# Sum of ReLU over rows: the first chunk in four loads of every fourth partition, and two row blocks instead of three

## The chip, the core and the metric

The kernel runs on one core of one Trainium2 chip. It uses ScalarE (ACT), VectorE (DVE) and SyncE (SP), which issues all transfers; TensorE has no part in it. The metric is the device time of one execution in microseconds, the median of several. The profile is one execution, taken by the hardware profiler; its times count from the start of its first instruction.

## The reference

```python
batch, seq, dim = 32, 512, 1024
x = np.random.randn(batch, seq, dim).astype(np.float32)

def reference(x):
    relu_x = np.maximum(x, 0)
    return np.sum(relu_x, axis=-1).astype(np.float32)
```

The input is 16384 rows of 1024 float32 numbers, 64 MB; the output is one number per row, 64 KB. Every number is read once.

## The kernel before

The rows are dealt to the 128 partitions of the on-chip buffer, 128 rows to each. `REGIONS = [1, 111, 16]` cuts the input into three row blocks. In a block of n, partition p holds the n consecutive rows from p*n on: in the first block one row (the first 128 rows of the input are contiguous over the partitions), in the second 111 rows (so that partition starts lie 444 KB apart), in the third 16 rows (64 KB apart).

Seven chunks of 16 rows per partition (64 KB per partition, 8 MB in all) go through three buffers of `buf`. Chunk 0 comes by two loads at L91, one of the first block's row (4 KB of each partition, 512 KB in all) and one of 15 rows of the second block (60 KB of each partition, 7680 KB in all). Chunks 1 to 6 are one load of 64 KB per partition each. All loads of a chunk count up the same semaphore, `s_in[c]`, by 16 each. The two loads of chunk 0 are moved in the instruction list ahead of SP's part in the start barrier, so they are issued first of all; chunks 1 and 2 follow behind the barrier, chunks 3 to 6 and the tail each wait until the DVE has finished with the buffer that they need (`s_dve`). The third block is the tail: loads of 8, 4 and 2 rows (L101), and two last rows in four pieces (three at L112, one at L115), one of which goes into a small buffer, `seam`.

On chunks 0 to 5, ACT applies ReLU in place to several rows at a time (L145) and the DVE sums them row by row into `res` (L160); in chunk 5 four rows are done outright by one engine each. From chunk 6 on, ACT (L127) and DVE (L130) take rows in turn, each with ReLU and sum in one operation. `res` has one column for each of the 128 rows of a partition.

The result goes out by three stores. Column 0 belongs to the first block, whose 128 results are contiguous in the output: after chunk 1 the DVE transposes the first 32 columns of `res` into `turned` (L169), and SP stores four rows of 32 numbers from there (L117). SP reaches this store behind all loads. The second block's 111 columns are stored at L123, once the last load of L112 has landed and chunk 6 is done, the third block's 16 columns at L207, once the last two sums are there. The program ends when all stores have landed.

Of the kernel before, what the change touches and what calls it, by code (L numbers as in the profile page):

```python
# [3 lines left out]
P = 128  # L4
D = 1024
BIG = 16
NB = 3
REGIONS = [1, 111, 16]
CHUNKS = [[(0, 0, 1), (1, 0, 15)]] + [[(1, 16 * c + 15, 16)] for c in range(6)]
ACT_STEPS = [[16], [7, 9], [7, 9], [7, 9], [4, 5, 7], [3, 4, 5]]  # L10
DVE_STEPS = [[4, 5, 7], [7, 4, 5], [7, 4, 5], [7, 4, 5], [4, 5, 7], [3, 4, 5]]
TAIL = [8, 4, 2]
# [4 lines left out]
def bass_relu_sum_kernel(  # L17
# [14 lines left out]
    fp32 = mybir.dt.float32  # L32
# [5 lines left out]
    J = B * S // P  # L38
    NBIG = len(CHUNKS)
    assert BIG * NBIG + sum(TAIL) + 2 == J == sum(REGIONS)  # L40

    xr = x.rearrange("b s d -> (b s) d")
    of = out.rearrange("b s -> (b s)")
    start = [sum(REGIONS[:i]) for i in range(len(REGIONS))]
    xv = [
        xr[P * s : P * (s + n), :].rearrange("(p j) d -> p j d", p=P)
        for s, n in zip(start, REGIONS)
    ]
    ov = [of[P * s : P * (s + n)].rearrange("(p j) -> p j", p=P) for s, n in zip(start, REGIONS)]

    buf = nc.alloc_sbuf_tensor("buf", [P, NB, BIG, D], fp32)
    w = D - CUT
    seam = nc.alloc_sbuf_tensor("seam", [P, 2 + w + HEAD + 2], fp32)
    res = nc.alloc_sbuf_tensor("res", [P, J], fp32)
    turned = nc.alloc_sbuf_tensor("turned", [P, 32], fp32)

    n_in = NBIG + len(TAIL) + 3
    s_in = [nc.alloc_semaphore(f"s_in{i}") for i in range(n_in)]
    s_act = nc.alloc_semaphore("s_act")
    s_dve = nc.alloc_semaphore("s_dve")  # L60
# [2 lines left out]
    s_half = nc.alloc_semaphore("s_half")  # L63
    s_seam = nc.alloc_semaphore("s_seam")
    s_last = nc.alloc_semaphore("s_last")
    s_turn = nc.alloc_semaphore("s_turn")
    s_store = nc.alloc_semaphore("s_store")
    s_out = nc.alloc_semaphore("s_out")

    sp, act, dve = nc.sync, nc.scalar, nc.vector  # L70

    NTWO = len(ACT_STEPS)
    done = [sum(map(len, DVE_STEPS[: c + 1])) for c in range(NTWO)]
# [5 lines left out]
    code = nc.main_func.blocks[0].instructions  # L79
    arrival = next(  # L80
        i
        for i, ins in enumerate(code)
        if ins.engine == mybir.EngineType.SP and type(ins).__name__ == "InstDrain"
    )
    for c in range(NBIG + 1):
        if c >= NB:
            sp.wait_ge(s_dve, done[c - NB])
        if c < NBIG:
            i = 0
            for g, j, n in CHUNKS[c]:  # L90
                sp.dma_start(  # L91
                    out=buf[:, c % NB, i : i + n, :], in_=xv[g][:, j : j + n, :]
                ).then_inc(s_in[c], 16)
                i += n
                if c == 0:
                    code.insert(arrival, code.pop())
                    arrival += 1
    r = 0
    tail = []
    for i, n in enumerate(TAIL):  # L100
# [10 lines left out]
    for k, (lo, hi) in enumerate((first, second, third)):  # L111
# [1 line left out]
            s_in[NBIG + len(TAIL) + k], 16  # L113
        )
    sp.dma_start(out=seam[:, 2 : 2 + w + HEAD], in_=rows[:, CUT : D + HEAD]).then_inc(s_seam, 16)  # L115
    sp.wait_ge(s_turn, 1)
    sp.dma_start(  # L117
        out=of[0:P].rearrange("(k q) -> k q", q=32), in_=turned[0:P:32, 0:32]
    ).then_inc(s_store, 16)
    sp.wait_ge(s_fact, 1)  # L120
    sp.wait_ge(s_fdve, 1)
    sp.wait_ge(s_in[-1], 16)
    sp.dma_start(out=ov[1][:, :], in_=res[:, start[1] : start[2]]).then_inc(s_store, 16)  # L123


    def on_act(t, acc):
        return act.activation(t, t, AF.Relu, accum_out=acc)  # L127

    def on_dve(t, acc):
        return dve.tensor_scalar(  # L130
            out=t, in0=t, scalar1=0.0, scalar2=None, op0=ALU.max, op1=ALU.add, accum_out=acc
        )

    def row(c, i):
        return buf[:, c % NB, i, :], res[:, c * BIG + i : c * BIG + i + 1]

    k = 0
    for c in range(NTWO):
        alone = BIG - sum(ACT_STEPS[c])
        act.wait_ge(s_in[c], 16 * len(CHUNKS[c]))  # L140
        r = 0
        ready = []
        for n in ACT_STEPS[c]:
            t = buf[:, c % NB, r : r + n, :]
            act.activation(t, t, AF.Relu).then_inc(s_act, 1)  # L145
            k += 1
            ready += [k] * n
            r += n
        for i in range(BIG - alone // 2, BIG):
            on_act(*row(c, i))  # L150
        if alone:
            dve.wait_ge(s_in[c], 16 * len(CHUNKS[c]))
            for i in range(BIG - alone, BIG - alone // 2):
                on_dve(*row(c, i))
        r = seen = 0
        for n in DVE_STEPS[c]:
            if ready[r + n - 1] > seen:
                seen = ready[r + n - 1]
                dve.wait_ge(s_act, seen)
            dve.tensor_reduce(  # L160
                out=res[:, c * BIG + r : c * BIG + r + n],
                in_=buf[:, c % NB, r : r + n, :],
                axis=X,
                op=ALU.add,
            ).then_inc(s_dve, 1)
            r += n
        if c == 1:
            dve.wait_ge(s_dve, done[c])
            dve.transpose(out=turned[:, :], in_=res[:, 0:32]).then_inc(s_turn, 1)  # L169


    j0 = NBIG * BIG
    for c in range(NTWO, NBIG):
        act.wait_ge(s_in[c], 16 * len(CHUNKS[c]))
        dve.wait_ge(s_in[c], 16 * len(CHUNKS[c]))
        for i in range(BIG):
# [15 lines left out]
    k = 2 + w  # L192
# [14 lines left out]
    sp.dma_start(out=ov[-1][:, :], in_=res[:, start[-1] : J]).then_inc(s_out, 16)  # L207
    sp.wait_ge(s_store, 16 * (len(REGIONS) - 1))
    sp.wait_ge(s_out, 16)
# [28 lines left out]
```

## Time and profile before

| | us |
|---|---|
| median of 3 runs | 160.88 (160.72 to 160.93) |
| span of the profiled execution, first to last instruction | 159.4 |
| DVE busy | 120.6 (76%) |
| ACT busy | 101.5 (64%) |
| input read, 67.11 MB, over the span | 421 GB/s |
| idle time of ACT until loads landed, L145 | 46.1 in 6 waits, 19.1 the longest |

The profiled execution's own time is its span; what a timed run has around it is the difference, 1.5 us. Instructions are named by engine, line, operation and tiles. "SPq" is SP's issuing of transfers; a load's "us to landing" counts from the start of its issue to its completion, including the time that it stands in the queues behind others.

### The profile page before, as it was taken

Reading aid. Unit: us, or ns where it says so; the run is one execution under the profiler, and the core shown is the slowest. Engines: PE = TensorE matmul, PEld = TensorE weight load, DVE = VectorE, ACT = ScalarE, POOL = GpSimd, SP = SyncE. Lnnn points to the kernel's source line nnn. Section 1 sums busy time; section 2 is a strip of 40 time slices with the busy share of each in tenths; the row PEclk is TensorE's granted clock in tenths of the full one; section 3 lists DMA queues with packets and bytes.
Section 4 is the critical chain, followed back from the end, with each engine's and each line's share of the span. In section 5 each row is a group of like instructions: output and inputs, shape, how many; then the busy total and the mean of one; then the engine's idle time right before and its main releaser. Section 6 shows DMA issues by size and latency. Waiting matters only on the chain.

```text
span 159.4 us, 150 instructions
## 1 busy us (share of the span) xinstructions
DVE 120.6 (76%) x59; ACT 101.5 (64%) x54; POOL 0.2 (0%) x4
## 2 busy tenths in 40 slices
DVE  0000000009999999999999999999999999898995
ACT  3000059980799708996099941999329980496975
POOL 0000000000000000000000000000000000000000
DMA  9997996996996997989979969969969979798994
GB/s 378 493 401 339 493 526 263 526 526 263 526 493 296 526 444 345 526 378 411 526 312 477 526 263 526 526 263 526 526 263 526 444 345 526 321 469 374 417 400 142
DMA packets 2457, 67.18 MB, mean 421 GB/s; under 512 B 536, under 2 KB 792, under 8 KB 1176
## 3 DMA queue, kind: packets, MB, share of 16 engines
q1 hardware_dynamic: 2456, 67.18, 98.1%
q14 instruction: 1, 0.01, 0.0%
HBM read 67.11 MB, written 0.07 MB: 421 GB/s over the span
## 4 chain that ended last, share of the span: by engine, by line
DVE 55%; DMA 34%; ACT 9%; SPq 2%; issue 0%
DVE res L160 54%; DMA buf<-in_x_dram 34%; ACT buf L145 9%; SPq L101 1%; SPq L112 1%; DVE buf L130 0%; DVE seam L130 0%; SPq L91 0%; DVE turned L169 0%
## 5 line engine op out<-in xcount | busy, mean ns | idle before, releaser
L160 DVE TENSOR_REDUCE res<-buf 128x4 f32<-128x4096 f32 (+3 forms) x18 | 99.4, 5596 | 35.5 <-ACT buf L145 35.5
L145 ACT ACTIVATE buf<-buf 128x7168 f32<-128x7168 f32 (+5 forms) x13 | 80.4, 6233 | 46.1 <-DMA buf<-in_x_dram 46.1
L127 ACT ACTIVATE buf<-buf 128x1024 f32<-128x1024 f32 (+2 forms) x19 | 19.0, 999 | 8.9 <-DMA buf<-in_x_dram 8.9
L130 DVE TENSOR_SCALAR_CACHE_REDUCE buf<-buf 128x1024 f32<-128x1024 f32 (+2 forms) x19 | 20.7, 1143 | 1.7 <-DMA buf<-in_x_dram 1.6
L127 ACT ACTIVATION_READ_ACCUMULATOR buf<-buf 128x1 f32 x19 | 3.6, 188 | 0.0
L145 ACT ACT_TABLE_LOAD x1 | 1.3, 1283 | 1.3 <-PEq L223 1.3
L130 DVE DVE_READ_ACCUMULATOR buf<-buf 128x1 f32 x19 | 1.6, 84 | 0.0
L130 DVE TENSOR_SCALAR_CACHE_REDUCE seam<-seam 128x258 f32<-128x258 f32 x1 | 0.4, 421 | 0.0
L127 ACT ACTIVATE seam<-seam 128x114 f32<-128x114 f32 x1 | 0.3, 300 | 0.1
L169 DVE STREAM_TRANSPOSE turned<-res 128x32 f32<-128x32 f32 x1 | 0.2, 211 | 0.0
L127 ACT ACTIVATION_READ_ACCUMULATOR seam<-seam 128x1 f32 x1 | 0.2, 186 | 0.0
L223 POOL MEMSET const-bfloat16-1.0<- 128x1 bf16 x1 | 0.1, 101 | 0.0
L223 POOL MEMSET const-uint8-127<- 128x1 uint8 x1 | 0.1, 101 | 0.0
L223 POOL MEMSET const-float32-0.0<- 128x1 f32 x1 | 0.1, 98 | 0.2 <-issue 0.2
L223 POOL MEMSET const-float32-1.0<- 128x1 f32 x1 | 0.1, 98 | 0.0
L130 DVE DVE_READ_ACCUMULATOR seam<-seam 128x1 f32 x1 | 0.1, 82 | 0.0
## 6 DMA issues: line engine op xcount, KB each, us to landing
buf<-in_x_dram SPq DMA_DIRECT2D x1, 7680.0 KB, 21.1
buf<-in_x_dram SPq DMA_DIRECT2D x1, 4096.0 KB, 25.3
buf<-in_x_dram SPq DMA_DIRECT2D x1, 2048.0 KB, 29.9
buf<-in_x_dram SPq DMA_DIRECT2D x1, 1024.0 KB, 31.9
buf<-in_x_dram SPq DMA_DIRECT2D x1, 512.0 KB, 3.3
buf<-in_x_dram SPq DMA_DIRECT2D x1, 456.0 KB, 32.5
buf<-in_x_dram SPq DMA_DIRECT2D x1, 256.0 KB, 32.7
seam<-in_x_dram SPq DMA_DIRECT2D x1, 184.0 KB, 32.6
```

What stands on the lines that cost most here:

```text
L101: sp.dma_start(out=buf[:, tb, r : r + n, :], in_=xv[-1][:, r : r + n, :]).then_inc(s_in[NBIG + i], 16)
L112: sp.dma_start(out=flat[:, lo:hi], in_=rows[:, lo:hi]).then_inc(s_in[NBIG + len(TAIL) + k], 16)
L127: return act.activation(t, t, AF.Relu, accum_out=acc)
L130: return dve.tensor_scalar(out=t, in0=t, scalar1=0.0, scalar2=None, op0=ALU.max, op1=ALU.add, accum_out=acc)
L145: act.activation(t, t, AF.Relu).then_inc(s_act, 1)
L160: dve.tensor_reduce(out=res[:, c * BIG + r : c * BIG + r + n], in_=buf[:, c % NB, r : r + n, :], axis=X, op=ALU.add,).then_inc(s_dve, 1)
L169: dve.transpose(out=turned[:, :], in_=res[:, 0:32]).then_inc(s_turn, 1)
L223: nc = _bacc.Bacc("TRN2", target_bir_lowering=False, num_devices=1)
```

## The change

There are two row blocks, `REGIONS = [112, 16]`: partition starts of the first lie 448 KB apart. All seven chunks are 16 rows of the first block. Chunk 0 comes by four loads; load q brings 64 KB to each of the partitions q, q+4, q+8, ..., 32 partitions each. All four are placed ahead of SP's part in the start barrier, and ACT waits for all four (64 counts). The transpose, its buffer, its semaphore and its store are gone; the store at the end takes 112 columns.

```diff
-REGIONS = [1, 111, 16]
-CHUNKS = [[(0, 0, 1), (1, 0, 15)]] + [[(1, 16 * c + 15, 16)] for c in range(6)]
+REGIONS = [112, 16]
+CHUNKS = [[(0, 16 * c, 16)] for c in range(7)]
+STEPS = [[4]] + [[1]] * 6
...
-            for g, j, n in CHUNKS[c]:
-                sp.dma_start(
-                    out=buf[:, c % NB, i : i + n, :], in_=xv[g][:, j : j + n, :]
-                ).then_inc(s_in[c], 16)
+            for (g, j, n), step in zip(CHUNKS[c], STEPS[c]):
+                for q in range(step):
+                    sp.dma_start(
+                        out=buf[q::step, c % NB, i : i + n, :], in_=xv[g][q::step, j : j + n, :]
+                    ).then_inc(s_in[c], 16)
+                    if c == 0:
+                        code.insert(arrival, code.pop())
+                        arrival += 1
                 i += n
-                if c == 0:
-                    code.insert(arrival, code.pop())
-                    arrival += 1
...
-    sp.wait_ge(s_turn, 1)
-    sp.dma_start(
-        out=of[0:P].rearrange("(k q) -> k q", q=32), in_=turned[0:P:32, 0:32]
-    ).then_inc(s_store, 16)
     sp.wait_ge(s_fact, 1)
     sp.wait_ge(s_fdve, 1)
     sp.wait_ge(s_in[-1], 16)
-    sp.dma_start(out=ov[1][:, :], in_=res[:, start[1] : start[2]]).then_inc(s_store, 16)
+    sp.dma_start(out=ov[0][:, :], in_=res[:, 0 : start[1]]).then_inc(s_store, 16)
...
-        act.wait_ge(s_in[c], 16 * len(CHUNKS[c]))
+        act.wait_ge(s_in[c], 16 * sum(STEPS[c]))
...
-        if c == 1:
-            dve.wait_ge(s_dve, done[c])
-            dve.transpose(out=turned[:, :], in_=res[:, 0:32]).then_inc(s_turn, 1)
```

More of the change, by code (lines that the diff above doesn't have):

```diff
@@ L54, in bass_relu_sum_kernel @@
     res = nc.alloc_sbuf_tensor("res", [P, J], fp32)
-    turned = nc.alloc_sbuf_tensor("turned", [P, 32], fp32)
     n_in = NBIG + len(TAIL) + 3
@@ L65, in bass_relu_sum_kernel @@
     s_last = nc.alloc_semaphore("s_last")
-    s_turn = nc.alloc_semaphore("s_turn")
     s_store = nc.alloc_semaphore("s_store")
@@ L151, in bass_relu_sum_kernel @@
         if alone:
-            dve.wait_ge(s_in[c], 16 * len(CHUNKS[c]))
+            dve.wait_ge(s_in[c], 16 * sum(STEPS[c]))
             for i in range(BIG - alone, BIG - alone // 2):
```

## The prediction

> **What bounds the kernel now.** I read the page first, then its part on DMA issues, the timeline, the table of stretches and the chain, and at the end the trace's record of single DMA packets for the first microseconds.
>
> The DMA row of the slices and the timeline (start us, us, engine, line, operation, tile, idle before it) settle the bound:
>
> ```profile
> span 159.4 us, 150 instructions
> DMA  9997996996996997989979969969969979798994
> ...
> 21.61 13.86 ACT L145 ACTIVATE buf<-buf 128x16384 f32<-128x16384 f32 x1 [19.06 <-DMA buf<-in_x_dram]
> 40.97 13.95 ACT L145 ACTIVATE buf<-buf 128x7168 f32<-128x7168 f32 x2 [5.50 <-DMA buf<-in_x_dram]
> 60.31 13.95 ACT L145 ACTIVATE buf<-buf 128x7168 f32<-128x7168 f32 x2 [5.39 <-DMA buf<-in_x_dram]
> 70.11 0.21 DVE L169 STREAM_TRANSPOSE turned<-res 128x32 f32<-128x32 f32 x1
> 137.72 1.22 DVE L130 TENSOR_SCALAR_CACHE_REDUCE buf<-buf 128x1024 f32<-128x1024 f32 x1 [0.42 <-DMA buf<-in_x_dram]
> 157.01 0.42 DVE L130 TENSOR_SCALAR_CACHE_REDUCE buf<-buf 128x256 f32<-128x256 f32 x1 [0.40 <-DMA buf<-in_x_dram]
> ```
>
> Every chunk of 8 MB is awaited by ACT, and chunks land 19.36, 19.34, ... us apart. The stretches (from:to, length, busy time of each engine, clock, DMA share, GB/s) say that nothing else limits that pitch:
>
> ```profile
> 21.60:40.97 19.37, 5.47 (x2) 13.86 (x2) 0.00 (x0) 1.00 1.00 433
> 40.97:60.31 19.34, 19.34 (x4) 13.95 (x3) 0.00 (x0) 1.00 1.00 434
> 60.31:79.67 19.36, 19.32 (x6) 13.96 (x3) 0.00 (x0) 1.00 1.00 433
> ```
>
> The queues are full (share 1.00) at 433.5 GB/s, 19.35 us a chunk. The DVE is as full, but as a follower: it starts when ACT has done chunk 0 and has 0.42 us to spare when chunk 6 lands at 137.72. The page's chain walks through the DVE and says otherwise:
>
> ```profile
> DVE 55%; DMA 34%; ACT 9%; SPq 2%; issue 0%
> ```
>
> It goes from the last data back to their issue at L101 (122.07), which waited for a DVE reduction. That is a wait of the issuing queue, not of the data: chunk 6 was still arriving until 137.72, so the tail's loads stood in the queue for some 15 us. The real chain is: start of the first load, 64 MB at a constant rate, 2.4 us of closing work. So the time moves one for one with the moment from which **all** DMA engines stream, and the change works there.
>
> The beginning, from the page's DMA issues (KB, us to landing):
>
> ```profile
> buf<-in_x_dram SPq DMA_DIRECT2D x1, 7680.0 KB, 21.1
> buf<-in_x_dram SPq DMA_DIRECT2D x1, 512.0 KB, 3.3
> ```
>
> Chunk 0 is complete at 21.59; a chunk takes 19.35 in the stream, so 2.24 us are start-up. The 512 KB load (4 KB of each partition) would take 1.21 us at the stream's rate and landed after 3.3: 2.1 us are issue, first access and landing. 7680 KB are 18.14 us, 3.3 + 18.14 = 21.44: another 0.15 was lost behind it.
>
> The packet record opens the 2.24 up. A packet is one partition's contiguous run, eight per DMA engine and load. The sixteen engines start their first 4 KB packet between 1.01 and 1.34 us. Those first packets last 362 ns on average, the others 175, the shortest 159; 4 KB at 27.1 GB/s (64 KB in 2418 ns) would be 151. The engines begin their 60 KB packets between 2.50 and 2.94 us, and this stagger of about 0.5 us stays to the end: the completion marks of chunk 0 arrive from 21.07 to 21.59, those of chunk 5 from 117.84 to 118.34. The slowest engine decides. The 60 KB packets last 2267 ns at best, the eight of one engine together lose 0.18 us to this.
>
> **The change, part by part** (gain positive, in us, for the slowest engine).
>
> 1. *No 4 KB packets.* Each engine now gets two 64 KB packets from each of four loads, 8 x 64 KB as before. Eight times the 8 ns of a small packet go: +0.06. The small packets' mutual delay, 7 x (175 - 159) ns, goes: +0.11. Bounds 0 and 0.31 (all that the 4 KB packets lost against 159 ns). The wait of each engine's first packet, 362 - 159 = 0.20, stays: 0.
> 2. *First load of 32 rows instead of 128.* The stagger of 0.33 between the engines' first packets may come from handing out eight rows to each engine in turn. With two rows it lies between 0.33 (no gain) and a quarter, 0.08 (gain 0.25). The stores at the end, eight rows per engine on a running queue, end within 0.14 to 0.15 us over all engines; so rows are part of it, not all. I take half: +0.13.
> 3. *Issue on SP.* Loads at L91 take 0.33 to 0.50 us; the one transfer whose partitions are stepped, the turned store at L117, took 0.63. If the step is what costs, each first packet comes 0.24 later than with the 0.39 of today's first issue. The four loads at 0.33 to 0.50 resemble the load rows more than a four-row store: 0, the loss end is -0.24. The second load is needed only when the first's two packets are through (4.8 us after its start), the others later; at 0.45 us apart they are queued by about 1.8 us.
> 4. *Two issues more ahead of SP's part in the start barrier*: the barrier ends some 0.9 us later. Behind it wait the table load of ACT (at 1.27, with 19.06 us of idle time after it) and the issue of chunk 1 (now at 1.28, needed at 20.7). Cost 0; without that cover 0.9.
> 5. *Two more completion marks per engine*, 9 ns each, with at most 0.03 for a change of load (19.35 less eight packet pitches of 2.4145): -0.02, end -0.06.
> 6. *Rows start 448 KB apart instead of 444.* The nearest row is the tail, 64 KB apart: all 128 of its 32 KB packets took exactly 1213 ns. The 64 KB packets of today's chunks take 2421 on average against 2418 at best, 0.03 per chunk. So 0 taken, gain end 0.16, loss end -0.18 (the excess of the cold first rows once more). That excess of 0.18 itself stays, since the first rows touched are again far apart.
> 7. *The transpose goes* (0.21 us at 70.11 and its wait on the DVE's own results). The DVE's slack at 137.72 grows from 0.42 to about 0.6; ACT and SP don't wait on it. 0. If the chunks came 0.4 faster with the DVE unmoved, the DVE would be late next; but it moves with chunk 0.
> 8. *The turned store goes from SP's queue* (0.63 at 125.35). Behind it SP only waits for the end's data, 31.0 us long. Its four 128 B packets lay behind all loads. 0. The 111 columns become 112: that store is issued at 157.08 and complete by 159.05, the last one, issued at 157.93, lands at 159.35 and sets the end. 0.
>
> Sum: 0.06 + 0.11 + 0.13 - 0.02 = 0.28. The span of 159.4 becomes 159.1. The timed median, 160.88 (160.72 to 160.93), has 1.5 us around the span that I leave alone: **160.6**. A change below 0.2%, 0.32 us, can't be told from none here.
>
> No row shows how 32 stepped partitions are dealt to the engines; the table of stretches has only full loads, at 433.5 GB/s. [...]
>
> **The rivals.**
>
> *A (slower): two engines share a way into the buffer during the first chunk.* In today's full loads each engine runs at 27.1 GB/s with no neighbour in its way. If the dealing of 32 rows sends two engines to partitions with one common path, both get half. Price: four loads at half rate are 38.7 instead of 19.35, 180 us in all; one load in four shared would be +4.8. It decides as soon as more than 0.6 us is lost (0.28 + 0.32): a quarter of one 64 KB packet of 2.42 us is then enough sharing. For it: nothing in the trace shows this shape. Against: the four loads together give every partition once, and the step of four spreads each of them over the whole buffer.
>
> *B (no gain): the start is latency.* First access (0.20), stagger (0.33) and issue remain, and the stepped issue costs 0.1 to 0.24: gain 0.17 less that, about 160.8.
>
> *C (more gain): the first packet comes sooner*, because fewer rows have to be prepared. The last 8 KB store lands 1.4 us after issue, so of 2.24 at most 0.84 can go: 160.0. With the full quarter stagger and the 0.16 of point 6: 160.3.
>
> **How the numbers follow.** Forecast case (sum between 0.15 and 0.45): 0.47, nearly split by the bound of 0.2%. C: 0.18. B, with small losses: 0.25. A: 0.10. Faster by over 0.2%: 0.18 + 0.22 = 0.40. Within: 0.25 of the forecast case + 0.17 of B = 0.42. Slower: 0.08 + 0.10 = 0.18. The range takes in B with its issue and row ends (160.88 + 0.24 + 0.06, about 161.2) and C to 160.1; it leaves out A and the edges, under 0.2.
>
> **What would show it.** Right: no 4 KB packets, the engines' first marks of the fourth load between 20.8 and 21.3, ACT's first operation at about 21.3 instead of 21.61, later pitches 19.35, everything behind moved by the same amount. Step 2 is wrong if the first packets still start over 0.33 us; step 3 if the first L91 issue takes over 0.5; step 6 if pitches leave 19.35. A would show as a first operation of ACT near 41, with DMA GB/s near 217 in the first slices. If ACT's first operation moves and the end doesn't, the DVE or the tail is the bound, and this reading is wrong.

## The result and the profile after

The changed kernel takes 161.82 us (five runs, 161.54 to 162.10) against 160.88 (160.72 to 160.93): slower, ratio 1.0062, 95% interval 1.0050 to 1.0073. That is 0.94 us more where 0.28 less was forecast, and beyond the upper end of the range. Ratios here and below hold fast runs against fast runs; only two runs of one variant, the 60 KB load stepped, are left out as slow.

The profiled execution has a span of 160.0 instead of 159.4, so 0.6 us of the loss lie inside it. The rest lies outside. The prediction took 1.5 us around the span from a median and the span of one execution; run by run, time less span is 1.36 us on average before (1.3 to 1.4 in fifteen runs) and 1.79 after (1.64 to 1.86 in five). So there are two losses to find: 0.56 us at the first chunk, 0.43 us around the span.

The page of the changed kernel (span, and the DMA row of the slices in tenths), answering to the lines shown of before:

```profile
span 160.0 us, 150 instructions
...
DMA  7997997999979969969969969969969979798994
```

It is as full as it was, but for the first slice (7 instead of 9). The timeline (start us, us, engine, line, operation, tile, idle before it):

```profile
22.17 13.86 ACT L141 ACTIVATE buf<-buf 128x16384 f32<-128x16384 f32 x1 [17.78 <-DMA buf<-in_x_dram]
41.49 6.18 ACT L141 ACTIVATE buf<-buf 128x7168 f32<-128x7168 f32 x1 [5.47 <-DMA buf<-in_x_dram]
...
138.25 1.22 DVE L126 TENSOR_SCALAR_CACHE_REDUCE buf<-buf 128x1024 f32<-128x1024 f32 x1 [0.61 <-DMA buf<-in_x_dram]
...
157.55 0.42 DVE L126 TENSOR_SCALAR_CACHE_REDUCE buf<-buf 128x256 f32<-128x256 f32 x1 [0.42 <-DMA buf<-in_x_dram]
```

ACT's first operation comes at 22.17 instead of 21.61, 0.56 later. From there nothing is won or lost: 41.49 is 0.52 later, 138.25 is 0.53, the last sums at 157.55 are 0.54. The stretches between chunks are as full as before:

```profile
22.16:41.49 19.33, 5.43 (x2) 13.86 (x2) 0.00 (x0) 1.00 1.00 434
41.49:60.85 19.36, 19.36 (x4) 13.95 (x3) 0.00 (x0) 1.00 1.00 433
```

The chain in order of time (start us, length, what) shows where the start went:

```profile
0.00 0.55 SPq L91
0.55 0.06 issue
0.60 0.58 SPq L91
1.18 0.04 issue
1.22 0.59 SPq L91
1.81 0.04 issue
1.86 20.29 DMA buf<-in_x_dram
```

Each stepped load takes 0.55 to 0.59 us to issue. The record of single packets adds that the sixteen DMA engines begin their first packet between 1.32 and 1.82 us (before: 1.01 to 1.34), and that these first 64 KB packets last 3.12 us on average where 2.418 is the best and the usual one: 0.70 lost by each engine on average. Before, a first 4 KB packet lost 0.20.

The second loss has its sign in the page's queue lines. Before:

```profile
q1 hardware_dynamic: 2456, 67.18, 98.1%
q14 instruction: 1, 0.01, 0.0%
```

After:

```profile
q1 hardware_dynamic: 2352, 67.18, 97.9%
```

Before, one packet of 8 KB of instructions was fetched within the span (at 159.21, the span ends at 159.39). After, no such packet is in it; the record has two, at 161.31 and 161.59, after the last profiled instruction at 159.96.

### The profile page after: what moved, and what is told of

It reads as the page before. It is cut to its first block, busy times and chain, and to the rows that moved or that the text cites. A ratio compares the mean times of both kernels' runs of the same rounds, so it can differ in the third digit from the quotient of the medians.

```text
span 160.0 us, 150 instructions
## 1 busy us (share of the span) xinstructions
DVE 120.4 (75%) x58; ACT 101.5 (63%) x54; POOL 0.2 (0%) x4
## 4 chain that ended last, share of the span: by engine, by line
DVE 55%; DMA 33%; ACT 9%; SPq 2%; issue 0%
DVE res L156 54%; DMA buf<-in_x_dram 33%; ACT buf L141 9%; SPq L91 1%; SPq L101 1%; SPq L112 1%; DVE buf L126 0%; DVE seam L126 0%
```

## The experiments

The table gives the runs. Medians are to be held against 160.81 to 160.88 of the kernel before, measured along with them. "Beyond" is time less span, the mean over the runs; "first packet" the start of the earliest one; "lost" what the engines' first packets lost on average against the best packet of the same size. All but the median and "beyond" come from one profiled execution each. Two pairs begin with the same loads, so they show how far single profiles scatter: ACT starts at 21.81 and 21.95 with one load, at 21.73 and 22.23 with 4 KB first, 448 KB apart.

| kernel | median | beyond | first issue at SP | first packet | lost | ACT starts |
|---|---|---|---|---|---|---|
| before | 160.86 | 1.36 | 0.39 | 1.01 | 0.20 | 21.61 |
| after | 161.82 | 1.79 | 0.55 | 1.32 | 0.70 | 22.17 |
| one load instead of four | 161.42 | 1.80 | 0.37 | 1.01 | 0.68 | 21.81 |
| two loads, every second partition | 161.76 | 1.73 | 0.55 | 1.34 | 0.61 | 22.05 |
| four loads of 32 neighbours | 183.24 | 1.90 | 0.39 | 1.02 | 2.54 | 43.27 |
| 4 KB first, 448 KB apart | 161.46 | 1.79 | 0.38 | 1.01 | 0.31 | 21.73 |
| before, 60 KB load stepped behind the 4 KB | 162.09 | 1.37 | 0.40 | 1.03 | 0.2 | 23.38 |
| before, 60 KB load first | 161.44 | 1.35 | 0.39 | 1.02 | 0.73 | 22.34 |
| before, a touch of the rows | 161.05 | 1.46 | 0.39 | 1.02 | 0.2 | 21.85 |
| after, two waits more on the DVE | 161.46 | 1.38 | 0.54 | 1.33 | 0.70 | 22.15 |
| 4 KB first, 448 KB apart, two waits more on the DVE | 161.08 | 1.38 | 0.38 | 1.01 | 0.45 | 22.23 |
| after, two waits more on ACT | 161.88 | 1.87 | 0.55 | 1.34 | 0.64 | 22.22 |
| one load, two waits more on the DVE | 161.05 | 1.37 | 0.37 | 1.00 | 0.71 | 21.95 |
| before, two DVE instructions less | 161.05 | 1.59 | 0.39 | 1.02 | 0.17 | 21.62 |

### One load instead of four

```diff
-STEPS = [[4]] + [[1]] * 6
+STEPS = [[1]] * 7
```

> The changed kernel with chunk 0 as one load of all 128 partitions, 64 KB each; blocks of 112 and 16 rows, no turned store. Three theories of the 0.56 us that ACT's first operation moved back (21.61 to 22.17). Issue: the stepped loads are slow to issue (0.55 us against 0.39), so the first packet comes at 1.32 instead of 1.01; here the issue is 0.33 to 0.42 and the first packet starts at 1.01. Cold: sixteen engines that begin with 64 KB packets in rows far apart lose 0.7 us each in the first packet (2418 ns at best); here the first packets still last 3.0 us or more, and ACT starts at 21.6 to 21.8. Crowding: the first packets are slowed by three more loads being prepared while they run; here they last under 2.6 us and ACT starts at about 21.2.

161.42 us, ratio to before 1.0041 (1.0029 to 1.0053). The issue is back at 0.37 and the first packet at 1.01; the first packets still last 3.09 us. ACT:

```profile
21.81 13.86 ACT L141 ACTIVATE buf<-buf 128x16384 f32<-128x16384 f32 x1 [19.76 <-DMA buf<-in_x_dram]
```

So stepping costs 0.36 at ACT (22.17 less 21.81) and 0.40 in the median. The long first packets are there with a single load, so crowding by the three others falls. What remains of ACT's delay against before is 0.20, with a first packet of 64 KB in place of the small contiguous load.

### Two loads of every second partition

```diff
-STEPS = [[4]] + [[1]] * 6
+STEPS = [[2]] + [[1]] * 6
```

> The changed kernel with two loads of every second partition instead of four of every fourth. Issue theory: the issue is slow because partitions are stepped, 0.55 us again, first packet at 1.3. If the issue's cost came from having fewer rows than 128, it would lie between 0.39 and 0.55. Cold theory: first packets last 3.0 us or more, ACT at 22.0 to 22.2. Crowding theory: one more load instead of three, ACT at about 21.8. The start barrier ends about 1.2 us earlier than with four loads; if the time beyond the span hangs on it, it lies between 1.5 and 1.8.

161.76 us (1.0053; 1.0041 to 1.0065). The issues take 0.55 and 0.57 with 64 rows as with 32. The chain in order of time begins so:

```profile
0.00 0.55 SPq L91
0.55 0.06 issue
0.61 21.42 DMA buf<-in_x_dram
```

The earlier barrier changes nothing beyond the span (1.73).

### Four loads of 32 neighbouring partitions

```diff
-                        out=buf[q::step, c % NB, i : i + n, :], in_=xv[g][q::step, j : j + n, :]
+                        out=buf[P // step * q : P // step * (q + 1), c % NB, i : i + n, :],
+                        in_=xv[g][P // step * q : P // step * (q + 1), j : j + n, :],
```

> The changed kernel with four loads of 32 neighbouring partitions instead of every fourth. Issue: if 0.55 us come from stepping the partitions, these issues take 0.33 to 0.42; if they come from 32 rows, 0.55 again. Sharing (rival A of the prediction, at its proper place): if engines share ways by neighbouring partitions, the packets last 4.8 us instead of 2.42, ACT starts near 41 and the span is 179; if not, ACT starts at 21.8 to 22.2.

183.24 us in two runs. Two things come apart here. The issues take 0.39 to 0.42 although they have only 32 rows each, one of them 0.52 when issued as the fourth. The chain begins so:

```profile
0.00 0.39 SPq L91
0.39 0.06 issue
0.44 0.42 SPq L91
0.86 0.04 issue
0.90 0.42 SPq L91
```

So the slow issue goes with the step (0.55 to 0.59 with 32 rows, 0.55 and 0.57 with 64), not with the number of rows. And here is the half rate of rival A of the prediction: the packets of the first chunk last 4.91 to 5.12 us on average instead of 2.42, and the slices show it (GB/s in 40 slices):

```profile
GB/s 231 231 231 231 231 217 202 58 217 419 289 448 462 462 462 462 462 419 303 433 462 462 462 462 462 419 303 433 462 462 462 462 462 419 303 433 462 394 391 155
```

In its timeline ACT starts at 43.27:

```profile
43.27 13.86 ACT L142 ACTIVATE buf<-buf 128x16384 f32<-128x16384 f32 x1 [39.70 <-DMA buf<-in_x_dram]
```

The first chunk runs at about half rate (231 GB/s against 433.5), later ones, over all partitions, at the full one (433 on average from the tenth to the 33rd slice). What the engines share in it, if anything, no run shows. The change's step of four has no such loss: from their third packet on, its engines lose nothing (2418 to 2422 ns).

### 4 KB first, in rows that lie apart

```diff
-CHUNKS = [[(0, 16 * c, 16)] for c in range(7)]
-STEPS = [[4]] + [[1]] * 6
+CHUNKS = [[(0, 0, 1), (0, 1, 15)]] + [[(0, 16 * c, 16)] for c in range(1, 7)]
+STEPS = [[1, 1]] + [[1]] * 6
```

> The changed kernel's blocks of 112 and 16 rows and no turned store, but chunk 0 by two loads over all partitions as before the change, 4 KB and then 60 KB of each partition; the first 4 KB now lie 448 KB apart instead of one behind the other. Cold theory: the 4 KB packets meet the far-apart rows first and last 0.5 us or more longer in all; the first load lands at 3.8 or later instead of 3.3 and ACT starts at 21.9 to 22.2. Issue and crowding theories: as before the change, landing at 3.3, ACT at 21.6, time within 0.2% of 160.88.

161.46 us (1.0036; 1.0024 to 1.0048). The first load lands at 3.63, 0.3 later than the contiguous one and less late than the cold theory said; then the 60 KB packets lose nothing at all (2267 to 2272 ns, against 0.18 us per engine before). Sum of both: ACT at 21.73, between the 21.61 of before and the 21.81 of one large load. Single profiles are too coarse to rank these starts, so the mean spans over all runs decide. They are 159.6 for this kernel and 159.7 for the one with one large load, and 159.7 for both when the DVE has two waits more, against 159.5 before. So small or large, a first load in rows that lie apart costs these kernels the same, 0.2 against before. Most of this kernel's loss of 0.6 us is again beyond the span.

### The 60 KB load stepped behind the contiguous one

```diff
+STEPS = [[1, 4]] + [[1]] * 6
...
-            for g, j, n in CHUNKS[c]:
...
+            for (g, j, n), step in zip(CHUNKS[c], STEPS[c]):
+                for q in range(step):
...
```

> The kernel before (blocks of 1, 111 and 16 rows, turned store), whose 60 KB load alone is replaced by four loads of every fourth partition; the contiguous 512 KB load stays first. Issue theory: the slow issues are hidden behind the first load's packets, ACT starts at 21.6 to 21.7. Crowding theory: the 60 KB packets start while loads are still being issued and lose 0.5 us or more, ACT starts at 22.1. Cold theory: as the issue theory. If the 0.3 us by which the changed kernel's timed runs grew beyond its span come from the later start barrier, the median grows by 0.3 here too although the span stays.

None of the three theories' numbers came. The ten runs scatter from 160.97 to 163.75, with a median of 162.09 and spans of 159.6 to 162.4; without the two longest the ratio is 1.0059 (1.0035 to 1.0084). In the profiled one (162.40) ACT starts at 23.38. Its fourth stepped issue took 1.27 us, and three engines began their 60 KB packets between 3.89 and 4.57 us, when the other thirteen had begun by 3.14; they stayed late to the end. What held them was not found. The expectation's last sentence is answered: the barrier ended 3.0 us later than before (ACT's table load at 4.24 instead of 1.27), and the time beyond the span stayed at 1.37.

### The order of the two loads reversed in the kernel before

```diff
-CHUNKS = [[(0, 0, 1), (1, 0, 15)]] + [[(1, 16 * c + 15, 16)] for c in range(6)]
+CHUNKS = [[(1, 0, 15), (0, 0, 1)]] + [[(1, 16 * c + 15, 16)] for c in range(6)]
...
-            i = 0
             for g, j, n in CHUNKS[c]:
+                i = 0 if c or not g else 1
...
```

> The kernel before with the two loads of chunk 0 in the other order: the 7680 KB of the 111-row block (60 KB per partition, 444 KB apart) first, the contiguous 512 KB second. Cold theory (a first packet in a far-apart row costs 0.7 us, whatever the pitch): the first 60 KB packets last about 2.9 to 3.0 us instead of 2.27, ACT starts at 21.75 to 21.9, as with the single 64 KB load at 448 KB (21.81); time 161.0 to 161.1. Rival, the pitch: if 448 KB were worse than 444, the first packets lose clearly less than 0.6 us here and ACT starts at 21.5 to 21.6, time 160.8.

161.44 us (1.0037; 1.0024 to 1.0051), more than either theory said. The first 60 KB packets last 2.99 us, 0.73 lost, at 444 KB as at 448: the pitch is not the reason. The expected 0.7 came, but also a stagger: the engines' completion of this load spreads over 1.02 us (20.05 to 21.08) instead of 0.5, and ACT starts at 22.34 instead of 21.9. Where the stagger comes from was not found. The 4 KB packets behind it lose nothing (159 ns each).

### A touch of the rows ahead of the loads

```diff
+    act.dma_start(out=touched[:, :], in_=xv[1][:, 0, 0:16]).then_inc(s_touch, 16)
+    code.insert(at_act, code.pop())
...
+    sp.wait_ge(s_touch, 16)
```

> The kernel before plus one small load issued from ACT ahead of the start barrier: 64 B from the first row of the 111-row block of each partition, into a buffer that nothing uses. Cold theory: the far-apart rows are touched while SP's first load is under way, the 60 KB packets lose nothing (0.18 us per engine before), as in the kernel whose 4 KB packets lay 448 KB apart; the touches cost up to 0.1; ACT starts at 21.5 to 21.6, time 160.7 to 160.9. Rival: what a first packet loses is not the rows' first touch but the engine's own start; then the 60 KB packets still lose 0.18 and ACT starts at 21.65 or later.

161.05 us (1.0012; 1.0003 to 1.0020), ACT at 21.85, the 60 KB packets lose 0.16 per engine. It decides nothing: the touches ran between 2.30 and 3.1 us, just as the 60 KB packets began, too late to have touched anything ahead of them.

### Two long-fulfilled waits on the DVE

```diff
+        if c == 1:
+            dve.wait_ge(s_act, 1)
+            dve.wait_ge(s_act, 1)
```

in the changed kernel, where the transpose and its wait had stood.

> The changed kernel with two more instructions in the DVE's list, waits that are long fulfilled, where the transpose and its wait stood; nothing else. The runs so far have 1.36 us beyond the span with the turned store and 1.7 to 1.8 without, and a fetch of 8 KB of instructions stands at 160.9 to 161.6, after the last instruction, where it is absent, but at 159.2 before the last instruction where it is present. Theory code length: the fetch hangs on the DVE's number of instructions; with two more it comes before the end, the time beyond the span falls to 1.36 and the median from 161.82 to about 161.4 with the span unchanged at 160.0. Rival, the store itself (a transfer less in SP's list): the time beyond the span stays at 1.8, median 161.8.

161.46 us (1.0035; 1.0021 to 1.0049). The span is what it was, the time beyond it falls from 1.79 to 1.38, and the line of the instruction queue is back on the page:

```profile
span 159.9 us, 151 instructions
...
q1 hardware_dynamic: 2352, 67.18, 97.9%
q14 instruction: 1, 0.01, 0.0%
```

The same two waits in the kernel with 4 KB first, 448 KB apart:

> The kernel of two loads, 4 KB and 60 KB, blocks of 112 and 16 rows, no turned store, with the same two fulfilled waits on the DVE. Theory code length: time beyond the span 1.36, span 159.5 to 159.6, median 160.9 to 161.0 instead of 161.46. Rival, the store itself: 161.4.

161.08 us (1.0012; 1.0003 to 1.0021), beyond the span 1.38 instead of 1.79. Its profiled execution had a span of 160.0, the others mostly 159.6 to 159.8.

### The same waits on ACT

```diff
+            act.wait_ge(s_in[0], 64)
+            act.wait_ge(s_in[0], 64)
```

> The changed kernel with the two fulfilled waits in ACT's list instead of the DVE's. If the time beyond the span hangs on the length of the DVE's list alone, it stays at 1.8 us and the median at 161.8; if any two more instructions on a working engine do it, 1.36 and 161.4.

161.88 us (1.0062; 1.0048 to 1.0076), beyond the span 1.87, against 1.38 with the two waits on the DVE. It is the DVE's list that matters here, not ACT's.

### Two DVE instructions less in the kernel before

```diff
-DVE_STEPS = [[4, 5, 7], [7, 4, 5], [7, 4, 5], [7, 4, 5], [4, 5, 7], [3, 4, 5]]
+DVE_STEPS = [[16], [7, 4, 5], [7, 4, 5], [7, 4, 5], [4, 5, 7], [3, 4, 5]]
```

> The kernel before, turned store and all, with chunk 0's sums on the DVE as one instruction of 16 rows instead of three of 4, 5 and 7: two instructions fewer in the DVE's list, as many as the change took out, the same work. Code length on the DVE: the fetch comes after the end, the time beyond the span grows from 1.36 to 1.8 us and the median from 160.85 to 161.3 with the span at 159.4 to 159.5. Rival, the turned store is what keeps the time beyond the span short: 1.36 and 160.85.

161.05 us (1.0011; 1.0002 to 1.0020) with the span at 159.5. The fetch moves behind the end (160.84), with the turned store in place. The time beyond the span grows to 1.59, half of the expected 0.43, between 1.35 and 1.75 in single runs.

Over all kernels the fetch has two places in the packet record. In six of the seven with a DVE list as long as before it begins 1.31 to 1.34 us after the DVE's last operation; in the seven with a shorter list, 1.33 to 1.37 us after the last instruction of the span. The time beyond the span is 1.35 to 1.46 in the first seven and 1.59 to 1.90 in the others. The one in between is the kernel with the loads reversed: its list is that of before, its fetch begins 0.12 us after the span's end, and it has 1.35. So the fetch's place is a sign that goes with the loss. That the fetch itself takes the time is not shown, as no record covers what happens there.

### One load and the two waits

> The changed kernel without the stepping (chunk 0 as one load of all partitions) and with the two fulfilled waits on the DVE. If the two causes found add up, the median is 161.82 less 0.42 (code) less 0.40 (stepped issue), 161.0, with 1.36 us beyond the span; if they overlap, it stays above 161.2.

161.05 us (1.0015; 1.0006 to 1.0024), beyond the span 1.37. The causes add up: 160.86 before; 0.2 for a first load in rows that lie apart in place of the contiguous 4 KB, 161.05; 0.41 for the step, 161.46; 0.36 for the DVE's list, 161.82. In the other order the list takes 0.37 (161.05 to 161.42) and the step 0.40. The first of the three is the least separated: between before and 161.05 the transpose, its store and the third row block go too. No version tried is faster than the kernel before.

## Why the prediction was wrong

*The bound* was right. The span moved with the moment from which all DMA engines stream, one for one to its end (0.56 at the first chunk, 0.54 at the last sums), and not by the DVE that the page's chain names first.

*Point 3, the issue on SP,* is the first step that failed. It set the loads of stepped partitions beside the other loads, 0.33 to 0.50 us, and took no cost, with the 0.63 of the stepped store as the loss end. The steps cost 0.55 to 0.59 with 32 and with 64 rows, and unstepped loads of 32 rows 0.39 to 0.42 (0.52 once). The row that was set aside as "a four-row store" was the nearest one in what mattered. Its end of 0.24 for the first packet was too low as well: that came 0.31 later than with one plain load, and ACT 0.36. Of the 0.31 the issue itself explains 0.18; the rest was not found.

*Point 1:* the small packets are gone, but the term "the wait of each engine's first packet, 0.20, stays" was mis-sized: a first 64 KB packet loses 0.70, and with 60 KB at the other pitch 0.73. Against what the 4 KB and 60 KB packets had lost together, the expected gain of 0.17 became a loss of 0.20 (one load without step against before). The long packet is not all of it, as 4 KB packets first, in rows that lie apart, cost the same 0.2 in the span. What a first long packet waits for was not settled: it is not the number of loads, not the pitch of 448 KB, and the touch came too late to test the rows.

*Point 2:* the stagger of the first packets did not shrink. It was 0.33 before, 0.49 with the four loads (0.84 when profiled again with the two waits on the DVE) and 0.58 with one load of 128 rows. Nothing of the gain of 0.13 came.

*The 1.5 us around the span "that I leave alone"* is the second failed step, and as large as the issue. Points 7 and 8 put the transpose's and the store's removal at nothing because no engine waits for them. That holds within the span: the DVE's slack grew from 0.42 to 0.61 as said, and nothing follows the store. But the transpose and its wait left the DVE's list, and with the shorter list the time beyond the span is 0.43 us longer; two waits that wait for nothing take 0.41 of it back. With it the fetch of 8 KB of instructions moves from the shadow of the last store to behind the end. In the kernel before, it begins within the span (159.21, the span ends at 159.39); after the change it does not (161.31, the last profiled instruction at 159.96), and whether it costs time there no run shows. Why the shorter list fetches later, and why the kernel before loses only half as much when it is shortened, was not found.

*Points 4, 5 and 6* were right in what they cost. ACT's table load moved from 1.27 to 3.10 with the barrier, 1.83 us where 0.9 was forecast, and nothing had to wait for it; completion marks take 9 ns on average; chunks land 19.35 us apart, (138.22 - 22.15) / 6, as before.

*The rivals.* B had the mechanism, latency at the start and a slow stepped issue, at 160.8; it lacked the first packet's 0.7 and all that lies around the span. A's half rate came in another kernel, four loads of neighbours, at 183 instead of its 180; that two engines share a way into the buffer there is not shown. C did not occur in any run: with 32 unstepped rows the first packet still came at 1.02.

## What to carry to other kernels

When one resource is full from the first chunk to the last, as the DMA queues were here (share 1.00 at 433 to 434 GB/s), only its first and last microsecond can be won, and there each issue and each engine's first packet counted: keep the first load plain (the stepped one cost 0.36 us at ACT, 0.40 in the median); of the starts tried, the small contiguous one remained the best (160.86 against 161.05 and more). For a moved or removed shape, look for the row that shares the property that changes (the step), not the one that shares the size. At differences below one per cent compare time less span run by run as well: a change that removes two instructions from an idle place can cost time outside the span that no line of the profile shows (here 0.43 us with the change, 0.23 with two sums less).

## What was not expected of the hardware

Loads over stepped partitions took 0.54 to 0.59 us to issue at the start of the program (1.27 once behind another load), plain ones of 32 rows 0.39 to 0.42 (0.52 once). The first long packet of each DMA engine loses 0.6 to 0.73 us in every kernel that begins with one and is fed in full, later ones 0.02 or less on average. Two instructions more or less in the DVE's list moved a fetch of 8 KB of instructions across the end of the span (from 159.21 to 161.31 with the change, to 160.84 with two sums less), and 0.2 to 0.4 us that no line of the span shows came or went with them. And 64 KB packets to 32 neighbouring partitions ran at half speed (4.91 to 5.12 us on average, 231 GB/s), those to every fourth one at full speed (2418 to 2422 ns from each engine's third on).
